# One layer of a hybrid streaming encoder: spatial products between the second gate's, attention loads for two pairs of heads, and cached rows' norms at the front

## The chip, the cores and the metric

The kernel runs on one core of one Trainium2 chip. The metric is the device time of one execution in microseconds (us). Before the change the median of three runs is 4267.01 us (4262.45 to 4268.91). TensorE does matrix products and transposes, VectorE and ScalarE work on their results, GpSimd issues the indirect gathers, and SyncE (SP) issues all other DMAs in one queue. TensorE's clock is granted at one of two levels, 1.2 and 2.4 GHz; the profile gives the granted clock as a share of the higher one.

## The reference

The layer takes 1024 new positions of a prompt stream (eight tiles of 128 rows) and 16 new positions of each of eight running streams (a ninth tile). All is float32, with a width of 1024. Cut to what matters here:

```python
h = rmsnorm(x, g_mix)
c_q, c_kv, k_r, z_u, z_v, z_ga, z_gb = split(h @ w_in)
# A: attention with 16 heads; keys of a running stream: 256 cached rows and 16 new ones
k_nope = rmsnorm((ckv_all @ w_uk).reshape(B, Sk, 16, 64), g_kn)
o_a = attend(q, k_nope, k_rope, ckv_all @ w_uv) @ w_oa
# B: spatial gating over chunks of 128 positions, 8 channel groups
u, v_g = gelu(z_u), rmsnorm(gelu(z_v), g_gm)
mixed = einsum('gts,bcsgd->bctgd', tril(w_s), v5) + b_s
o_b = (u * mixed) @ w_ob
x = x + (sigmoid(z_ga) * o_a + sigmoid(z_gb) * o_b) @ w_o
x = x + cross_attend(rmsnorm(x))          # 256 memory rows, 4 heads
x = x + peer_ffn(rmsnorm(x))              # 8 heads pick 16 of 16384 experts each
```

A prompt tile attends to its own tile and the tiles before it. In the last step each row scores two sets of 128 keys per head, takes the best 16 pairs, and sums the picked experts.

## The kernel before, in words

**Groups and stages.** The nine tiles go through the layer in four groups: (0, 8), (1, 2), (3, 4, 5) and (6, 7); tile 8 holds the running streams. `mixer` (from L1430) runs for each group: `projections`, `attend_prompt`, for group 0 `attend_sample`, `merge`, `cross`, the latents of the next group and `pre_route`. Group 0 also computes the memory's keys and values in between (`memory`). After the last group, `dense_layer` treats tiles 2 to 5 by running all 16384 experts over them as dense products; the experts of tiles 0, 8, 1, 6 and 7 are gathered row by row by GpSimd and summed on VectorE, beside everything else.

**What sets the order.** The code is traced in program order, and a scheduler then fixes the order of each engine's queue and SP's at compile time: what stands earlier goes first, unless its inputs or tiles are not there yet by the scheduler's own estimate. At run time each queue is served strictly in its order. Work from the last group's expert choice (`route`, with its `tails`), from the gathers and from the scatter of the picks is dealt out between the products of the next group by `pump` (L181), which compares counters of planned time with a clock that each product advances (`mm`, L158). `force_route` (L218) takes a step of the route without waiting for that clock; `open` counts the routes whose query products (`ppq`) are not all out.

**Tiles.** Pools have a fixed number of places: twelve general tiles of 128x1024 (`mid`, L261), four activation tiles (`act_slot`, L285), three weight tiles of 1 MB (`weight`, L273), one tile `cqT` (`spare`, L264), and in PSUM four banks `mm`, two `tr` and two `s` (L270). A load whose place is taken waits, and so does all that stands behind it in SP's queue.

**Cached rows' norms** (`past_norms`, L457). The keys of the 8 x 256 cached rows are never stored; only the inverse norm of each of their 16 heads is. For each block of 128 rows `key_squares` (L449) makes two products of 128x512 from w_uk and the cached rows (two halves each), squares them on ScalarE and sums by head on VectorE. It is a generator; `attend_prompt` takes two of its sixteen steps with every pair of heads of group 0. The result (`own`, in the place of `cqT`) is used in `attend_sample`, which also loads the new rows' own values into that tile.

**Spatial part** (`projections`, L677 to L702). For each of eight channel groups g, one product per prompt tile with the masked spatial weights (`pmix`), scaled and shifted on VectorE into `mx` (L684, L689) and multiplied into `uT` (L691). After all eight, bT takes an activation tile, and for each of eight blocks of columns come eight products of the gate (`pg`, w_gb), a Sigmoid into a small tile (L699), eight products of the result (`po`, w_ob), and the product of the two on VectorE (L701).

**Attention of the prompt** (`attend_prompt`, L747). A unit is one head of one tile; two heads are a pair. In each step of the pipeline one unit's scores are made and its softmax is started, the probabilities of the unit two back are transposed, and the values of the pair three back are summed. `load(hp)` (L755) fetches the queries (qts), the keys of both heads (kts, two loads) and the values (vts) of one pair of heads; the next pair is asked for in the middle of a pair. `fill` deals the 64 steps of the first gate (`gate`, L704, w_ga) over the units. Group 0 has one prompt tile with one tile of keys, group 1 two with up to three.

Of the kernel before, what the change touches and what calls it, by code (L numbers as in the profile page):

```python
# [16 lines left out]
ALU = mybir.AluOpType  # L17
# [119 lines left out]
class Net:  # L137
# [319 lines left out]
    def past_norms(self):  # L457

        self.own = self.spare("own")
        self.rpast = self.own[:, :16 * H].rearrange("p (c h) -> p c h", c=16)  # L460
        wk = self.weight('w_uk', 0)

        def load(b):
            ck = self.mid("ckp", 512).rearrange("p (k t) -> p k t", k=2)
            self.dma(ck, self.A['past'][b, :, :2])
            return ck

        cks = [load(0)]
        for b in range(NST):
            if b + 1 < NST:  # L470
                cks.append(load(b + 1))
            ck = cks[b]
            for i in range(2):
                self.key_squares(self.rpast[:, 2 * b + i], ck[:, :, i * P:(i + 1) * P], wk)
                yield
        r = self.rpast
        self.nc.scalar.activation(r, r, AF.Sqrt, bias=self.eps)
        self.nc.vector.reciprocal(r, r)
# [76 lines left out]
    def projections(self, tiles, hT, lat, r):  # L555
# [108 lines left out]
        if SAMPLE in tiles:  # L664
# [9 lines left out]
            for b in range(NST):  # L674
                self.dma(trs[b * STOK:(b + 1) * STOK, :, b * STOK:(b + 1) * STOK], A['wsT'][:STOK, :, :STOK])
            nc.vector.tensor_tensor(trs, trs, bc(self.tril[:, None, :], [P, 8, P]), op=ALU.mult)
        for g in range(8):  # L677
            pm = self.psum("mm", "pmix")
# [12 lines left out]
            nc.vector.tensor_tensor(uT[:, g, :], uT[:, g, :], mx[:, :T], op=ALU.mult)  # L691
        bT = self.act_slot("bT", T)
        for c in range(4):
            wg, wo = self.weight('w_gb', c), self.weight('w_ob', c)
            for b in range(2):
                pg, po = self.psum("mm", "pg"), self.psum("mm", "po")
                self.mmT(pg[:, :T], hT, wg, b)
                sg = self.small("sg", TMAX, "row", 2)[:, :T]
                nc.scalar.activation(sg, pg[:, :T], AF.Sigmoid)  # L699
                self.mmT(po[:, :T], uT, wo, b)  # L700
                nc.vector.tensor_tensor(bT[:, 2 * c + b, :], po[:, :T], sg, op=ALU.mult)  # L701
        return bT  # L702
# [43 lines left out]

    def attend_prompt(self, tiles, oT, filler, gate):  # L747
        nc = self.nc
        ts = [t for t in tiles if t != SAMPLE]
        if not ts:  # L750
            return
        n, nk = len(ts), ts[-1] + 1
        st, ld = {}, {}

        def load(hp):  # L755
            hs = slice(2 * hp, 2 * hp + 2)
            qt = self.mid("qts").rearrange("p (h t k) -> p h t k", h=2, t=4)
            self.dma(qt[:QKD, :, :n], self.qd[:, hs, ts[0]:nk])
            kt = []
            for h in range(2):  # L760
                k = self.mid("kts").rearrange("p (t k) -> p t k", t=8)
                self.dma(k[:QKD, :nk], self.kd[:, 2 * hp + h, :nk])
                kt.append(k)
            vt = self.mid("vts").rearrange("p (t v) -> p t v", t=8)
            self.dma(vt[:, :nk], self.vd[:, :nk, hp * P:(hp + 1) * P])
            ld[hp] = qt, kt, vt

        def scores(u):
            hp, i, h = u
            if hp not in ld:  # L770
                load(hp)
            if 2 * i + h == n and hp + 1 < H // 2:
                load(hp + 1)
            qt, kt, vt = ld[hp]
            t = ts[i]
            chunks = []
            for c in range(0, t + 1, 4):
                m = min(4, t + 1 - c)
                s = self.psum("mm" if (c > 0 or (t < 4 and h)) else "s", "s")
                self.mm(s[:, :m * P].rearrange("p (t k) -> p t k", t=m), qt[:QKD, h, i, :],  # L780
                        kt[h][:QKD, c:c + m, :], start=True, stop=True)
                if c + m == t + 1:
                    nc.vector.memset(s[:64, m * P - 64:m * P], NEG)
                chunks.append(s[:, :m * P])
            st[u] = self.softmax(chunks, "pr")
# [4 lines left out]
        def values(u):  # L790
            hp, i, h = u
            if not h:
                return
            vt, t = ld[hp][2], ts[i]
            po = self.psum('tr', "pov")
# [6 lines left out]
        def fill(u):  # L802
            fill.due += 64 / len(units)
            while fill.due >= 1:
                next(gate, None)
                fill.due -= 1
            if u[1:] == (0, 0):
                next(filler, None)
                next(filler, None)

# [619 lines left out]
    def mixer(self, ctx):  # L1430
# [6 lines left out]
        groups = [list(g) for g in self.groups]  # L1437
        hT = self.head(groups[0], *self.inputs(groups[0]))
        lat = self.latents(groups[0], hT)
        for gi, tiles in enumerate(groups):  # L1440
# [4 lines left out]
            gate = self.gate(tiles, hT, sa)  # L1445
            while self.open:
                self.force_route()
            if gi == 0:
                self.memory()
            oT = self.act_slot("oT", T)  # L1450
            norms = iter(self.past_norms()) if SAMPLE in tiles else iter(())
            self.attend_prompt(tiles, oT, norms, gate)
            for _ in norms:
                pass
            if SAMPLE in tiles:
# [55 lines left out]
```

## Time and profile before

| | |
|---|---|
| Runs | 4267.01 us median (4262.45 to 4268.91) |
| Profiled execution | 4245.56 us, its span 4243.8 us |
| Mean granted clock of TensorE | 0.948 |
| TensorE busy | 3855.5 us (91%) |
| VectorE busy | 3281.3 us (77%) |
| ScalarE busy | 1466.4 us (35%) |
| GpSimd busy | 1660.5 us (39%) |
| HBM | 283 GB/s over the span |

The stages follow each other along TensorE's queue: group 0 until about 610 us, group 1 until about 1100, group 2 until about 1850, group 3 until about 2660, then the dense experts, which end near 4180, and the rest of the gathers. A busy TensorE is not one at its peak: the same product takes twice as long while the lower clock is granted. Idle time of an engine counts only where the chain that ends last runs through it.

### The profile page before, as it was taken

What the parts mean: (1) busy time and instruction counts of PE and PEld (TensorE: products, weight loads), DVE (VectorE), ACT (ScalarE), POOL (GpSimd) and SP (SyncE); (2) the same over time, 40 slices, a digit from 0 to 9 for tenths busy, and PEclk for the clock granted to TensorE, in tenths of its full rate; (3) what the DMA queues carried; (4) which work ended last, traced back from release to release, by engine and by line L of the source; (5) the groups of instructions that cost most, each with busy time, mean ns of one, the idle gap of its engine ahead of it and who ended that gap; (6) DMA issues with size and microseconds to landing.
All of it is one profiled execution on the core that took longest, in us unless ns stands there. A gap on an engine that the chain in (4) does not pass through costs nothing. (4 is left out here: it accounts for less than half of the span.)

```text
span 4243.8 us, 55015 instructions
## 1 busy us (share of the span) xinstructions
PE 3855.5 (91%) x18532; PEld 2930.3 (69%) x18532; DVE 3281.3 (77%) x7539; ACT 1466.4 (35%) x2987; POOL 1660.5 (39%) x1284
## 2 busy tenths in 40 slices
PE   8999999889997899989878887889999999999994
PEld 6856767767754566656655666667888878888883
DVE  2121138756897888789898887899999989999999
ACT  4153234162241384314156441332332332332330
POOL 0000000434434456543223332246666555666555
PEclk9997999989998999999889998899999999999997
DMA  6532465878878899897778885779999999999998
GB/s 204 176 114 72 150 211 181 332 244 316 329 271 297 287 301 354 302 350 285 244 232 255 272 290 209 270 254 368 346 363 371 342 335 356 362 346 357 359 326 329
DMA packets 456027, 1205.55 MB, mean 284 GB/s; under 512 B 48896, under 2 KB 180032, under 8 KB 432320
## 3 DMA queue, kind: packets, MB, share of 16 engines
q0 software_dynamic: 184320, 671.17, 44.0%
q1 hardware_dynamic: 271424, 530.86, 36.2%
q8 instruction: 147, 2.41, 0.2%
q14 instruction: 136, 1.11, 0.1%
HBM read 1131.04 MB, written 70.82 MB: 283 GB/s over the span
## 5 line engine op out<-in xcount | busy, mean ns | idle before, releaser
L1211 POOL DMA_INDIRECT v<-peer_v,e x640 | 879.3, 1374 | 1251.4 <-DVE dots L1228 807.9
L1211 POOL DMA_INDIRECT u<-peer_u,e x640 | 780.9, 1220 | 1320.2 <-DMA e<-ed 739.5
L1250 DVE SCALAR_TENSOR_TENSOR acc<-v,wk,acc 128x1024 f32<-128x1024 f32 x635 | 814.1, 1282 | 8.5 <-DMA v<-peer_v,e 6.5
L1228 DVE CUSTOM_DVE_ANT_0 u<-u,hx 128x1024 f32<-128x1024 f32 x640 | 776.8, 1219 | 24.4 <-DMA u<-peer_u,e 24.2
L163 PE MATMUL pu<-hh,uh 128*128 128x512 f32 x1024 | 410.7, 401 | 6.6 <-ACT uh L290 4.3
L163 PE MATMUL pd<-vl,ph 128*128 128x512 f32 x1024 | 403.8, 394 | 6.0 <-DVE vl L1345 6.0
L163 PE MATMUL pu<-hl,uh 128*128 128x512 f32 x1024 | 401.7, 392 | 0.0
L163 PE MATMUL pd<-vh,pl 128*128 128x512 f32 x1024 | 401.4, 392 | 0.0
L163 PE MATMUL pd<-vh,ph 128*128 128x512 f32 x1024 | 383.2, 396 | 11.2 <-DVE dy L1420 8.4
L290 ACT ACTIVATE vh<-v 128x512 fp32r<-128x512 f32 x256 | 161.5, 632 | 604.8 <-PE pd L163 294.9
L163 PE MATMUL pg<-hT,w 128*128 128x256 f32 (+1 forms) x1024 | 296.4, 423 | 7.5 <-ACT pr L732 4.8
L163 PE MATMUL ppq<-h3T,w 128*128 128x256 f32 (+1 forms) x1024 | 262.7, 415 | 3.6 <-ACT sc L290 2.7
L163 PE MATMUL pu<-hh,ul 128*128 128x512 f32 x1024 | 261.9, 395 | 1.9 <-DVE ul L1345 1.7
L163 PEld LDWEIGHTS ppq<-h3T,w 128*128 128x128 f32 x1024 | 195.8, 194 | 62.5 <-ACT sc L290 9.8
L163 PEld LDWEIGHTS pd<-vh,ph 128*128 128x128 f32 x1024 | 193.1, 189 | 58.3 <-DVE dy L1420 9.5
L163 PEld LDWEIGHTS pg<-hT,w 128*128 128x128 f32 x1024 | 190.1, 197 | 59.2 <-issue 13.4
L163 PEld LDWEIGHTS pd<-vl,ph 128*128 128x128 f32 x1024 | 193.5, 189 | 52.2 <-DVE vl L1345 13.1
L163 PEld LDWEIGHTS pu<-hh,uh 128*128 128x128 f32 x1024 | 193.6, 189 | 48.4 <-ACT da L1396 4.8
L163 PEld LDWEIGHTS pu<-hh,ul 128*128 128x128 f32 x1024 | 194.0, 190 | 44.6 <-DVE ul L1345 4.2
L163 PEld LDWEIGHTS pd<-vh,pl 128*128 128x128 f32 x1024 | 193.6, 189 | 40.1
L163 PEld LDWEIGHTS pu<-hl,uh 128*128 128x128 f32 x1024 | 193.6, 189 | 38.2
L163 PEld LDWEIGHTS <-sa 128*128 128x128 bf16 x1536 | 114.0, 104 | 147.0 <-DVE sa L1323 71.6
(284 smaller groups left out, 6955.8 us busy)
## 6 DMA issues: line engine op xcount, KB each, us to landing
u<-uT SPq DMA_DIRECT2D x128, 512.0 KB, 7.1
v<-peer_v SPq DMA_DIRECT2D x256, 256.0 KB, 7.2
w<-w_pq SPq DMA_DIRECT2D x32, 1024.0 KB, 7.2
gd<-stage SPq DMA_DIRECT2D x256, 128.0 KB, 4.4
dg<-gd SPq DMA_DIRECT2D x128, 256.0 KB, 7.1
w<-w_zv SPq DMA_DIRECT2D x16, 1024.0 KB, 6.4
w<-w_zu SPq DMA_DIRECT2D x16, 1024.0 KB, 7.2
w<-w_gb SPq DMA_DIRECT2D x16, 1024.0 KB, 8.1
```

Source lines behind the costliest of these rows:

```text
L163: i = self.nc.tensor.matmul(out, lhsT, rhs, **k)
L290: self.nc.scalar.activation(out, in_, AF.Copy, **k)
L1211: i = self.nc.gpsimd.indirect_dma_start(out=q, out_offset=None, in_=src, in_offset=bass.IndirectOffsetOnAxis(ap=idx, axis=0))
L1228: self.after(nc.vector.tensor_tensor_reduce(u, u, hx, 1.0, 0.0, ALU.mult, ALU.add, accum_out=dots[:, k:k + 1]))
L1250: i = nc.vector.scalar_tensor_tensor(acc, v, w[:, k:k + 1], acc, op0=ALU.mult, op1=ALU.add)
```

## The change

The norms of the cached rows become a plain function that is called before the head of the first group, right after its inputs are asked for; their tile comes from the general ones. In the attention they no longer stand between the units. Where a group has at most two prompt tiles and at most four tiles of keys (groups 0 and 1), one load of queries, keys and values covers two pairs of heads (`w = 2`); each of the four loads is then twice as large, and the next is asked for in the middle of the two pairs. In the spatial part each channel group's products are followed by the eight products of one block of the gate, whose Sigmoid goes straight into bT; the products with w_ob follow when all eight are through and multiply bT in place. bT is taken ahead of that loop, and so is the loop that forces the open routes to their end.

```diff
     def past_norms(self):
-        self.own = self.spare("own")
+        self.own = self.mid("own")
...
                 self.key_squares(self.rpast[:, 2 * b + i], ck[:, :, i * P:(i + 1) * P], wk)
-                yield
...
     def projections(self, tiles, hT, lat, r):
...
+        while self.open:
+            self.force_route()
+        bT = self.act_slot("bT", T)
         for g in range(8):
             pm = self.psum("mm", "pmix")
...
             nc.vector.tensor_tensor(uT[:, g, :], uT[:, g, :], mx[:, :T], op=ALU.mult)
-        bT = self.act_slot("bT", T)
+            if g % 2 == 0:
+                wg = self.weight('w_gb', g // 2)
+            pg = self.psum("mm", "pg")
+            self.mmT(pg[:, :T], hT, wg, g % 2)
+            nc.scalar.activation(bT[:, g, :], pg[:, :T], AF.Sigmoid)
         for c in range(4):
-            wg, wo = self.weight('w_gb', c), self.weight('w_ob', c)
+            wo = self.weight('w_ob', c)
             for b in range(2):
-                pg, po = self.psum("mm", "pg"), self.psum("mm", "po")
-                self.mmT(pg[:, :T], hT, wg, b)
-                sg = self.small("sg", TMAX, "row", 2)[:, :T]
-                nc.scalar.activation(sg, pg[:, :T], AF.Sigmoid)
+                po = self.psum("mm", "po")
                 self.mmT(po[:, :T], uT, wo, b)
-                nc.vector.tensor_tensor(bT[:, 2 * c + b, :], po[:, :T], sg, op=ALU.mult)
+                nc.vector.tensor_tensor(bT[:, 2 * c + b, :], po[:, :T], bT[:, 2 * c + b, :], op=ALU.mult)
...
-    def attend_prompt(self, tiles, oT, filler, gate):
+    def attend_prompt(self, tiles, oT, gate):
...
         n, nk = len(ts), ts[-1] + 1
+        w = 2 if n <= 2 and nk <= 4 else 1
...
-        def load(hp):
-            hs = slice(2 * hp, 2 * hp + 2)
-            qt = self.mid("qts").rearrange("p (h t k) -> p h t k", h=2, t=4)
-            self.dma(qt[:QKD, :, :n], self.qd[:, hs, ts[0]:nk])
+        def load(l):
+            hs = 2 * w * l
+            qt = self.mid("qts").rearrange("p (h t k) -> p h t k", h=2 * w, k=P)
+            self.dma(qt[:QKD, :, :n], self.qd[:, hs:hs + 2 * w, ts[0]:nk])
             kt = []
             for h in range(2):
-                k = self.mid("kts").rearrange("p (t k) -> p t k", t=8)
-                self.dma(k[:QKD, :nk], self.kd[:, 2 * hp + h, :nk])
-                kt.append(k)
-            vt = self.mid("vts").rearrange("p (t v) -> p t v", t=8)
-            self.dma(vt[:, :nk], self.vd[:, :nk, hp * P:(hp + 1) * P])
-            ld[hp] = qt, kt, vt
+                k = self.mid("kts").rearrange("p (h t k) -> p h t k", h=w, k=P)
+                self.dma(k[:QKD, :, :nk], self.kd[:, hs + w * h:hs + w * (h + 1), :nk])
+                kt += [k[:, e] for e in range(w)]
+            vt = self.mid("vts").rearrange("p (t v) -> p t v", v=P * w)
+            self.dma(vt[:, :nk], self.vd[:, :nk, l * w * P:(l + 1) * w * P])
+            ld[l] = qt, kt, vt
...
-            if hp not in ld:
-                load(hp)
-            if 2 * i + h == n and hp + 1 < H // 2:
-                load(hp + 1)
-            qt, kt, vt = ld[hp]
+            l, o = hp // w, hp % w
+            if l not in ld:
+                load(l)
+            if 2 * (n * o + i) + h == n * w and l + 1 < H // 2 // w:
+                load(l + 1)
+            qt, kt, vt = ld[l]
+            h += 2 * o
...
-            if u[1:] == (0, 0):
-                next(filler, None)
-                next(filler, None)
...
-        hT = self.head(groups[0], *self.inputs(groups[0]))
+        first = self.inputs(groups[0])
+        if SAMPLE in groups[0]:
+            self.past_norms()
+        hT = self.head(groups[0], *first)
...
-            while self.open:
-                self.force_route()
             if gi == 0:
                 self.memory()
             oT = self.act_slot("oT", T)
-            norms = iter(self.past_norms()) if SAMPLE in tiles else iter(())
-            self.attend_prompt(tiles, oT, norms, gate)
-            for _ in norms:
-                pass
+            if SAMPLE in tiles and gi:
+                self.past_norms()
+            self.attend_prompt(tiles, oT, gate)
```

## Rows read from the trace of the kernel before

**Rows 1.** Busy time, granted clock and DMA of five stretches (PEclk 1.00: 2.4 GHz), by window.

```profile
core 0: us, PE busy (x) PEld busy (x) DVE busy (x) ACT busy (x) POOL busy (x), PEclk, DMA share, GB/s
...
218.00:315.00 97.00, 92.29 (x331) 55.07 (x330) 31.11 (x81) 59.79 (x130) 0.00 (x0) 0.99 0.36 106
...
835.00:940.00 105.00, 84.24 (x444) 59.90 (x443) 48.37 (x142) 71.60 (x167) 29.19 (x26) 0.85 0.77 253
...
1306.00:1345.00 39.00, 22.27 (x85) 15.42 (x84) 37.80 (x76) 4.41 (x7) 18.70 (x16) 0.69 0.72 262
...
2700.00:4180.00 1480.00, 1452.50 (x6537) 1184.62 (x6536) 1417.17 (x1997) 444.79 (x636) 857.74 (x649) 0.99 0.94 342
...
2625.00:2650.00 25.00, 20.07 (x106) 16.86 (x104) 15.05 (x99) 5.00 (x13) 0.00 (x0) 1.00 0.06 17
```

**Rows 2.** Timeline of the start, a weight's landing, and the norms' matmuls in the attention.

```profile
3.37 0.43 SPq L257 DMA_DIRECT2D w<-w_ckv  x1
...
14.42 3.93 PE L177 MATMUL pt<-const,xn 128*128 128x128 f32 x16 [14.42 <-ACT xn L290]
...
w<-w_pq SPq DMA_DIRECT2D x32, 1024.0 KB, 7.2
...
218.18 7.03 PE L163 MATMUL pk<-w,ckp 128*128 128x512 f32 x16
225.05 1.89 PE L163 MATMUL pg<-hT,w 128*128 128x256 f32 x8
```

**Rows 3.** Group 0's attention: costliest groups, TensorE's last wait, landing of its keys.

```profile
L353 ACT ACTIVATE sq<-pk 128x512 f32<-128x512 f32 x32 | 18.0, 597 | 34.8 <-PE pk L163 17.7 <-PE s L163 17.1
...
L732 ACT ACT_TABLE_LOAD x8 | 10.3, 1283 | 0.4 <-DVE s L783 0.3
...
314.72 7.16 PE L163 MATMUL pqa<-qq,wkT 64*128 64x128 f32 x32 [0.79 <-DMA qq<-qd]
...
DMA to landing us min/median/max: 1.8/1.9/6.5
```

**Rows 4.** Group 1's attention: TensorE's waits, one late load, landing of its keys.

```profile
PE s L163 <- DMA kts<-kd: 19.8, 5, 6.7
...
876.45 0.36 SPq L257 DMA_DIRECT2D w<-w_oa  x1
...
877.32 1.10 SPq L257 DMA_DIRECT2D kts<-kd  x2
...
887.62 4.60 PE L163 MATMUL s<-kts,qts 96*128 96x256 f32 x8 [4.48 <-DMA kts<-kd]
...
DMA to landing us min/median/max: 2.1/2.3/13.2
```

**Rows 5.** TensorE's waits at the spatial products (whole run, group 2, group 3); its timeline in group 2.

```profile
PE pmix L163 <- DVE mx L684: 24.1, 7, 13.2
...
PE pmix L163 <- DVE mx L684: 16.6, 3, 13.2
...
PE pgs L163 <- DVE sa L1323: 7.1, 4, 6.1
PE pmix L163 <- DVE mx L684: 5.0, 2, 2.8
...
1332.34 7.39 PE L163 MATMUL pg<-hT,w 128*128 128x384 f32 x16
...
1340.21 0.27 PE L177 MATMUL pt<-const,efij 128*128 128x128 f32 x1
```

**Rows 6.** VectorE at the spatial products of groups 2 and 3, timeline.

```profile
1321.54 0.61 DVE L684 SCALAR_TENSOR_TENSOR mx<-pmix,gcol,bs_p 128x384 f32<-128x384 f32 x1
...
1322.55 0.55 DVE L691 TENSOR_TENSOR uT<-uT,mx 128x384 f32<-128x384 f32 x1
...
2063.85 0.29 DVE L1322 TENSOR_TENSOR so<-iotas,pk 128x256 bf16<-128x256 bf16 x1 [6.83 <-DMA pk<-pb]
```

**Rows 7.** The route's query products alone, by window: group 2's spatial products.

```profile
1306.00:1345.00 39.00, 0.00 (x0) 0.69 0.72 262
```

More of the change, by code (lines that the diff above doesn't have):

```diff
@@ L778, in scores @@
                 m = min(4, t + 1 - c)
-                s = self.psum("mm" if (c > 0 or (t < 4 and h)) else "s", "s")
+                s = self.psum("mm" if (c > 0 or (t < 4 and h % 2)) else "s", "s")
                 self.mm(s[:, :m * P].rearrange("p (t k) -> p t k", t=m), qt[:QKD, h, i, :],
@@ L793, in values @@
                 return
-            vt, t = ld[hp][2], ts[i]
+            vt, t = ld[hp // w][2][:, :, hp % w * P:], ts[i]
             po = self.psum('tr', "pov")
```

## The prediction, before the change was run

> **What bounds the kernel now.** I read the stretches first, by window. In the dense stretch, 2700 to 4180 us, TensorE is busy 1452.5 of 1480 us, and nothing of it is touched; before it, at 2625 us, GpSimd has no gather left and VectorE is idle 10 of 25 us [rows 1]. So nothing is carried across that point but the place of TensorE's chain: what TensorE's chain gains or loses before it moves the end by as much. That makes the sum one of TensorE's time, stage by stage, where it is idle or slow. Then the start and the stretch in which the norms run now [rows 2, 3]: TensorE does nothing until 14.42 us, and in the attention of group 0 it is 92.29 of 97 us busy, because the norms' products pad it. Then group 1's attention, which has no such padding: 84.24 of 105 us busy, at a granted clock of 0.85, and the longest wait is for the keys [rows 1, 4]. Then the spatial products, where TensorE waits 24.1 us in all for VectorE, 16.6 in group 2 and 5.0 in group 3 [rows 5], and what VectorE did meanwhile [rows 6]. The profiled execution took 4245.6 us, 21 us under the median of the runs (4267.0). I make the sum on its span and take the difference over to the median. A measurement of this kernel can tell about 0.2% (8.5 us) from no change.
>
> **Norms at the start.** The same 64 products (128 instructions) move from group 0's attention to the front. Sixteen take 225.05 - 218.18 = 6.87 us [rows 2], so all take 8 x 6.87 = 55.0 us, at the full clock that the start has now too. Before, TensorE waited until 14.42 us for the normalised input. The norms need only w_uk and the first cached rows: asked for where w_ckv is now, at some 3.4 to 4 us, a 1 MB weight needs 7.2 us (its median), so they start near 11 us and fill 3.4 us of the wait [rows 2]. Bounds: nothing filled (the queue is crowded with inputs) and 7.2 us (the weight lands 7.2 us into the span). **Cost: +55.0 - 3.4 = +51.6 us** (48 to 55). What covered them before was the attention; that cover is gone from here. SP's queue gets w_uk and eight loads of cached rows ahead of the latents' weights, which have 55 us to land. The tile that holds the norms now keeps one of the twelve general tiles until the cached streams' attention is over; the products it would starve are loads ahead of a TensorE that has work, so I cost it at nothing, and up to 5 us if that cover fails.
>
> **Group 0's attention without them.** From the first norm product to the first product of the cached streams it takes 314.72 - 218.18 = 96.5 us [rows 2, 3]. Left are 92.29 - 55.0 = 37.3 us of TensorE and 59.79 - 18.0 = 41.8 us of ScalarE [rows 1, 3]. ScalarE is then the longer engine, and each score waits for it through the softmax, so the floor is 42 us. The ceiling is all of TensorE's work at 1.2 GHz, 75 us. The nearest row is group 1's attention: without its key waits it took (105 - 19.8) / 71.6 = 1.19 of ScalarE's busy time [rows 1, 4]. 41.8 x 1.19 = 50 us, which I take. The loads take 1.9 us here (median) [rows 3] and come half as often, so they hide. **Gain: -46.5 us** (-22 to -54). With the norms, group 0 comes to +5 us: it moves work more than it saves any. ScalarE's floor holds sixteen table loads, eight before Exp and eight before the gate's Sigmoid, at 1.283 us each [rows 3]. The Trainium skill (ScalarE: Activation LUTs, Table sets: the hidden batching unit) wants all calls of one set done before the next and gives about 2.7 us to a switch; by that figure the floor would be 64 us and the change some 20 us worse, but the rows say 1.283 and the measurement decides.
>
> **Short loads in pairs.** Only groups 0 and 1 are short enough; groups 2 and 3 keep their loads. In group 1 a pair's keys are asked for two units ahead, and queue behind a 1 MB weight: requested at 877.32, behind w_oa, used at 887.62 after a wait of 4.48 us [rows 4]. The waits sum to 19.8 us in five places. Now one request in two remains, and it comes four units ahead. A unit takes (105 - 19.8) / 32 = 2.7 us, so the lead goes from 5 to 11 us, against the 10 us that this load took (887.62 - 877.32) and 13.2 at most. Three boundaries at 1 to 2 us leave about 4: -16 us. The granted clock of 0.85 is 30% of 105 us, 31 us, at 1.2 GHz; at most 31 - 20 = 11 of these were work, and work at half speed loses half, 5.7 us. I take back 3. **Gain: -19 us**; bounds 0 (the loads are as late as now) and -25.5. SP issues fewer requests (16 fewer per group); the bytes are the same.
>
> **Spatial products with the gate's.** Nothing is added; the gate's eight products (one per channel group) stand between the spatial ones and give VectorE time. Groups 0 and 1 wait 24.1 - 16.6 - 5.0 = 2.5 us in all, and lose that: -2.5. In group 2 VectorE reaches the first result at 1321.54, some 15 us late, being behind with gathers and with the route's tail, and is busy 37.8 of 39 us [rows 1, 6]. Two spatial and two gate products can now run before TensorE needs a bank back, about 12 us of work by the gate's 7.39 us at a mixed clock [rows 5]. That would save 12. But the route's transposes come next: TensorE takes one at 1340.21, and it needs VectorE's index work, which now stands behind eight pairs of 0.61 + 0.55 us [rows 5, 6]. With six of these moved behind it, it is ready at 1340 - 7 = 1333, and TensorE will be there at about 1318 and wait. At 1333 it has then done two gate products (10 us) for the six spatial ones (4 us) that it has yet to do. **I take -4** (0 to -16.6). Group 3 is the same with another blocker: the scatter's products wait 7.1 us for tiles that VectorE can't build until a load of the picks lands at 2063.85 [rows 5, 6]. That load doesn't come sooner, and TensorE meets its products sooner. **I take -2** (0 to -12). The forced end of the route, moved ahead of the spatial products, costs nothing: none of its query products lies in that window [rows 7], so none is left to force; were some left, each would be 16 products in a row. The fourth activation slot is then free too. Gate values written straight into the result's tile save no instruction.
>
> **Sum:** 51.6 - 46.5 - 19 - 2.5 - 4 - 2 = **-22.4 us**, 4223 on the profiled execution, **4245 us** against the median.
>
> **The rivals.**
> 1. The spatial waits vanish whole (the index work and the picks are done in time after the reordering): 12.6 + 10 more, -45, 4222 us. For it: the waits are the longest single ones there. Against: VectorE is saturated in that window.
> 2. Group 1's gain is taken up elsewhere: in 85 us instead of 105, 71.6 us of ScalarE and a DMA share of 0.77 become 0.84 and 0.95 [rows 1]; gathers then land late and hold VectorE's queue ahead of the softmax. -22.4 + 19 = -3, 4264 us.
> 3. Group 0's attention, with its padding gone, runs at 1.2 GHz: 75 instead of 50 us, +25, sum +3, 4270 us. For it: in group 1 the clock is at 0.85 where TensorE waits [rows 1]. Against: there it waits for DMAs of 10 us, here for chains of one or two. The Trainium skill (TensorE: Matmul & The Clock Gate, HAM oscillation) says that idle gaps bring the half clock and that the matmuls behind them start slow; it speaks against taking filler out of a stage.
> 4. Slower: the tiles decide. A pair of pairs needs four free tiles out of twelve (eleven in group 0). If prefetched requests must wait for tiles of the set in use, all four loads leave only after its last score, and every boundary pays the whole landing: in group 1 three of 13.2 us in place of 19.8, and no gain, 19 + 19.8 = +39 against my term; in group 0 three of 6.5, +19.5. Sum -22 + 58 = +36, 4303 us; if only group 1 pays, 4284. It decides from the point where the second keys of a set are requested after the last score of the set before. Against: of twelve tiles, four are loaded and three to five hold probabilities at that time, so three or more are free.
>
> **Chances.** The forecast 0.52 (its own range 4230 to 4258), rival 1 0.16, rival 2 0.16, rival 3 0.05, rival 4 0.11. Faster by over 0.2% takes the forecast and rival 1, a little less for the forecast's upper edge: 0.67; rivals 2 and 3 are the same: 0.21; slower 0.12. The range 4214 to 4278 leaves out rival 4 and the better half of rival 1.
>
> **What would show it.** TensorE's first product near 11 us and 55 us of norms; group 0's attention of about 50 us with ScalarE over 80% busy; key waits in group 1 of about 4 us and a clock over 0.9; no wait at a spatial product in group 1, and in groups 2 and 3 waits for index or scatter tiles instead. I am wrong where group 0's attention is over 60 us or under 45, where group 1 still waits over 15 us for keys, or where groups 2 and 3 gain over 15 us.

## The result, and the profile after

The changed kernel takes 4207.65 us, median of five runs (4196.05 to 4237.43), against 4267.01 (4262.45 to 4268.91, five runs too): a ratio of 0.9872, 95% interval [0.9832, 0.9913], which is 37 to 72 us less (55 by the ratio itself). I had forecast 22 us less. The profiled execution took 4237.43 us, the longest of the five, its span 4235.7: only 8.1 us under the span of before. So the two profiles seem to say one thing and the medians another. That is resolved first, since everything else is read from profiles.

The page of the changed kernel, its head and the granted clock over 40 slices:

```profile
span 4235.7 us, 54898 instructions
...
PE 3874.7 (91%) x18532; PEld 2949.3 (70%) x18532; DVE 3282.5 (77%) x7539; ACT 1462.5 (35%) x2985; POOL 1656.1 (39%) x1284
...
PEclk9996699999999899999898998899999999999997
```

One slice is 106 us. The 6 and 6 at the fourth and fifth are the attention over the cached streams (`attend_sample`), which the change doesn't touch. The stages, by window (columns as in [rows 1]):

```profile
275.00:318.00 43.00, 37.33 (x201) 29.52 (x199) 9.19 (x49) 40.48 (x96) 0.00 (x0) 0.93 0.57 176
318.00:493.60 175.60, 162.40 (x673) 122.06 (x672) 20.12 (x65) 45.28 (x166) 0.00 (x0) 0.60 0.21 64
...
866.00:930.00 64.00, 62.70 (x379) 48.12 (x378) 45.02 (x132) 58.62 (x139) 22.40 (x23) 1.00 0.99 323
...
1305.00:1363.00 58.00, 46.35 (x162) 28.71 (x161) 53.23 (x100) 8.53 (x15) 35.24 (x29) 0.88 0.89 332
```

Group 0's attention fell to 43 us (first line; [rows 1], 97 with the norms). Group 1's attention is at the full clock with TensorE busy throughout (third line; 0.85 and 84.24 of 105 us in [rows 1]). The streams' stage has the opposite: 175.6 us at 0.60. In the profile of before it took 144.1 us, with the same 673 matmul instructions.

**The stages over all profiles.** I took the start of the first instruction of each stage on TensorE from every trace (first scores, first `pqa`, first product with w_oa, first `pmix`, last product with w_ob, last scores) and subtracted. "Streams" runs from the first `pqa` to the first product with w_oa. The columns are the profile of before and of the change, the change run again (e5), and parts of it: norms alone (e1), loads alone (e2), spatial alternation alone (e3), loads and spatial (e4), alternation in group 2 alone (e11) and in group 1 alone (e12).

| us | before | change | e5 | e1 | e2 | e3 | e4 | e11 | e12 |
|---|---|---|---|---|---|---|---|---|---|
| to group 0's first scores | 226.8 | 274.9 | 275.8 | 277.0 | 226.9 | 224.4 | 225.7 | 227.3 | 226.6 |
| group 0's attention | 87.9 | 43.1 | 43.0 | 46.1 | 88.8 | 87.7 | 87.5 | 88.0 | 88.0 |
| streams | 144.1 | 175.6 | 165.1 | 153.9 | 157.1 | 152.4 | 170.3 | 175.6 | 163.4 |
| group 1, spatial part | 67.8 | 68.1 | 68.2 | 68.0 | 67.1 | 60.1 | 68.4 | 69.7 | 60.2 |
| group 1, attention | 94.6 | 64.5 | 63.7 | 91.0 | 63.0 | 82.5 | 62.9 | 102.0 | 80.0 |
| group 2, spatial part | 141.3 | 124.6 | 123.3 | 150.1 | 151.2 | 122.9 | 123.1 | 126.8 | 147.4 |
| group 2, attention | 188.3 | 197.5 | 195.1 | 188.3 | 187.7 | 197.5 | 194.2 | 197.3 | 188.9 |
| group 3, spatial part | 99.0 | 100.8 | 100.7 | 96.0 | 98.6 | 96.6 | 97.2 | 94.7 | 92.2 |
| span | 4243.8 | 4235.7 | 4225.0 | 4259.8 | 4229.3 | 4207.8 | 4223.2 | 4262.2 | 4234.5 |
| span less streams | 4099.7 | 4060.1 | 4059.9 | 4105.9 | 4072.2 | 4055.4 | 4052.9 | 4086.6 | 4071.1 |

The streams' row moves between 144 and 176 us with no relation to what was edited: e11, which touches only group 2 a thousand microseconds later, has 175.6, as the change has. It is the same code in all nine columns. The profiled execution of before has the shortest stage of them. Without it, the change and its repetition come to 4060.1 and 4059.9, **39.7 us under before**, inside the interval of the medians. That they agree to 0.2 us is in part luck: in the rows of the table above it they differ by 3.7 us, and what the rows leave out makes up for it. That last row is what I compare below, beside the medians, and it scatters too. Group 2's spatial part, unaltered, takes 141.3 to 151.2 us, group 1's attention 91.0 to 102.0, and what the rows leave out, code that no edit changes, comes to 3181 us (e11) to 3194 (before and e4). So only 32 of the change's 39.7 us lie in the rows that the table shows (36 in e5), and a difference under some 13 us in the last row has to be looked for in the rows of the edited stages.

### The profile page after: what moved, and what is told of

It is laid out like the page before. It is cut to its first block, busy times and chain, and to the rows that moved or that the text cites. A ratio compares the mean times of both kernels' runs of the same rounds, so it can differ in the third digit from the quotient of the medians.

```text
span 4235.7 us, 54898 instructions
## 1 busy us (share of the span) xinstructions
PE 3874.7 (91%) x18532; PEld 2949.3 (70%) x18532; DVE 3282.5 (77%) x7539; ACT 1462.5 (35%) x2985; POOL 1656.1 (39%) x1284
## 5 line engine op out<-in xcount | busy, mean ns | idle before, releaser
L163 PEld LDWEIGHTS pg<-hT,w 128*128 128x128 f32 x1024 | 193.1, 201 | 67.1 <-issue 19.4
L163 PEld LDWEIGHTS pd<-vl,ph 128*128 128x128 f32 x1024 | 192.8, 188 | 52.0 <-DVE vl L1348 13.2
L163 PEld LDWEIGHTS pd<-vh,pl 128*128 128x128 f32 x1024 | 192.9, 188 | 39.7
```

The source lines that it names most:

```text
L163: i = self.nc.tensor.matmul(out, lhsT, rhs, **k)
```

## The experiments

### One part of the change at a time

The norms alone (e1), the loads alone (e2), the spatial part alone (e3), loads and spatial part without the norms (e4), and the whole change once more (e5). Each edit is the hunks of the change's diff that belong to that part, with nothing else; their marks:

```diff
# e1
+        if SAMPLE in groups[0]:
+            self.past_norms()
-            norms = iter(self.past_norms()) if SAMPLE in tiles else iter(())
# e2
+        w = 2 if n <= 2 and nk <= 4 else 1
# e3
+            pg = self.psum("mm", "pg")
+            self.mmT(pg[:, :T], hT, wg, g % 2)
+            nc.scalar.activation(bT[:, g, :], pg[:, :T], AF.Sigmoid)
# e4: e2 and e3; e5: the whole change
```

> The norms at the front alone, the rest as before. Theory A (the clock in the cached streams' stage decides group 0): the stretch up to that stage ends within 8 us of before (the change's profile shows +3.3), the stage itself takes between 125 and 180 us by its granted clock (145 at 0.78 before, 177 at 0.60 in the profile of the change), and the executions differ among themselves by more than 20 us, where those of before differ by 6; the median lies between 20 us faster and 30 us slower. Theory B (group 0 is settled, and the rest of the change makes the gain): a stage within 5 us of before, executions within 10 us of each other, and 0 to 5 us slower.

> The attention's loads for two pairs alone. Theory A: group 1's attention gains what the profile of the change shows there beside the spatial products, 25 to 30 us, and some of it is lost again before the end: 15 to 30 us faster, with executions within 10 us of each other since group 0's filler stands where it stood. Theory B (whatever group 1 gains is waited for later, as group 3 started at the same time in both profiles): under 5 us faster.

> The spatial products between the gate's alone. Theory A: 2 to 5 us gained in group 1, 15 to 18 in group 2 by the end of its spatial part, given back to under 5 by the end of that group, nothing in group 3: 0 to 10 us faster in all. Theory B (the spatial waits are the gain that the profiled execution hides): 15 to 30 us faster.

> The change without the norms' move (loads and spatial products only). Theory A: the sum of the two parts, 20 to 40 us faster, executions within 10 us of each other; the change beats it only where the cached streams' stage has the higher clock. Theory B (the norms' move is what makes the gain of the median): under 15 us faster.

> The changed kernel once more, beside the kernel before on the same chip. Theory A (the change is the sum of its parts, -31 for the loads and -23 for the spatial products, overlapping in group 1 to -38 together, and 0 to +15 for the norms): 25 to 40 us faster than before (0.6 to 0.9%). Theory B (the parts help each other, as the first measurement of 1.28% says): 50 us or more faster. In its profile group 1's attention takes 63 to 66 us at full clock, and group 0 reaches the cached streams within 8 us of before.

Measured, each against the kernel before on the same chip: e1 4268.2 us, ratio 1.0035 [1.0008, 1.0063]; e2 4224.05, 0.9926 [0.9895, 0.9957]; e3 4227.33, 0.9946 [0.9917, 0.9974]; e4 4212.77, 0.9905 [0.9872, 0.9939]; e5 4218.92, 0.9889 [0.9862, 0.9917].

- **e1:** the norms' move costs a little, 0.08 to 0.63% (3 to 27 us), and 6.2 us by the last row of the table. One half of theory A holds: the streams' stage began 8.3 us later than before (323.0 against 314.7), as the two rows above it say. The other half fell: it wanted executions of before within 6 us of each other, and on this chip before itself went from 4229.9 to 4285.05.
- **e2:** 0.43 to 1.05% (18 to 45 us), 27.5 us by the table. Group 1's attention went from 94.6 to 63.0 us. Its window in e2:

```profile
846.00:909.00 63.00, 62.95 (x378) 47.35 (x377) 43.64 (x130) 58.28 (x137) 28.02 (x24) 1.00 1.01 341
```

TensorE has no idle time left and the full clock throughout. Theory A's 15 to 30 us holds; its executions within 10 us of each other did not come (4215.11 to 4231.11).

- **e3:** 0.26 to 0.83% (11 to 35 us), and 44.3 us by the last row. The interval leaves out theory A's 0 to 10 and holds theory B's 15 to 30, the one against my forecast. The table shows 29.0 us of it in three places: 7.7 us in group 1's spatial part, 12.1 in its attention, which the edit doesn't contain, and 18.4 in group 2's spatial part, of which 9.2 are given back in the attention behind it. Most of the other 15 us lies in stages that the edit does not reach.
- **e4:** the parts do not add up. In group 1, loads and alternation together (68.4 + 62.9 = 131.3 us) are no better than the loads alone (67.1 + 63.0 = 130.1). The whole is 0.61 to 1.28% faster (26 to 54 us), so theory A's sum holds at its upper end and theory B's under 15 us is out; the executions lie 30 us apart (4201.73 to 4231.78), not within 10.
- **e5:** 0.83 to 1.38%, 35 to 59 us, between the two theories' figures.

### Where the alternation pays: group 2 alone (e11), group 1 alone (e12)

```diff
+        alt = len(tiles) == 3        # e12: alt = tiles[0] == 1
+        if alt:
+            while self.open:
+                self.force_route()
+            bT = self.act_slot("bT", T)
         for g in range(8):
...
+            if not alt:
+                continue
```

with the change's loop where `alt` holds and that of before elsewhere.

> The kernel before, with the spatial products alternated with the gate's in group 2 alone (with the forced end of the route and bT ahead of them there). Theory A (the failed step is group 2's: TensorE does gate products in the 17 us in which it waited, at a higher clock): group 2's spatial part 120 to 130 us where it was 141, 6 to 9 us given back in the attention after it, and span less the streams' stage 8 to 15 us under the before kernel's 4099.7. Theory B (as I predicted: the transposes take the place of the wait): spatial part 135 to 141 us, gain under 5 us.

> The kernel before, with the alternation in group 1 alone. Theory A (in group 1 it pays through what follows: the gate's weights are asked for earlier, the result's products run together, and the attention behind waits less for its keys): from the first spatial product to the last product with w_ob 58 to 64 us where it was 68, the attention behind it 80 to 88 us where it was 95, span less the streams' stage 15 to 25 us under 4099.7. Theory B (as I predicted: only the waits of 2.5 us at the spatial products go): spatial part 65 to 68 us, attention 92 or more, gain under 5 us.

e11: 4245.7 us, 0.9953 [0.9925, 0.9982]; e12: 4234.73, 0.9917 [0.9880, 0.9955]. In its stages theory A came out in both: e11's group 2 takes 126.8 us in the spatial part and gives back 9.0 in the attention behind it, and e12's two stages take 60.2 and 80.0. The last row says less: e11 is 13.1 us under before, but its rows add up to what they were before (905.8 and 905.7 us; group 1, which it does not touch, took 9.3 us longer, group 2 was 5.5 shorter), so the 13.1 us lie outside its rows. The runs themselves give e11 8 to 32 us. Of e12's 28.6 us, over A's 15 to 25, 22.2 lie in group 1. TensorE's waits in group 2's spatial part and the attention behind it, in e11:

```profile
PE pt L177 <- DVE efij L1188: 6.1, 1, 6.1
PE pmix L163 <- DVE mx L689: 4.7, 1, 4.7
PE pgs L163 <- DVE sa L1343: 3.6, 1, 3.6
```

The 16.6 us at `mx` [rows 5] became 4.7, and 6.1 turned up at the transposes of the route, as forecast in kind. In size it was not. Both windows of group 1 in e12, and its waits:

```profile
779.00:839.00 60.00, 58.68 (x288) 51.96 (x287) 52.25 (x115) 6.32 (x12) 29.20 (x24) 1.00 0.96 363
839.00:919.00 80.00, 69.76 (x378) 51.83 (x378) 44.29 (x129) 58.67 (x139) 24.55 (x23) 0.91 0.85 272
```

```profile
PE s L163 <- DMA kts<-kd: 9.1, 3, 4.8
PE pg L163 <- DMA w<-w_gb: 1.3, 1, 1.3
```

The alternation also changes the order of SP's queue (four w_gb together, then four w_ob), and the key waits in the attention behind fell from 19.8 to 9.1 us in three places. That the order of the queue brings this was not tried by itself, nor was the alternation without that order. That gain and the doubled loads' are of the same waits, which can be removed only once. With both edits the spatial part itself keeps 68 us; another load is late then. The changed kernel, its wait in group 1's spatial part:

```profile
PE pg L163 <- DMA w<-w_gb: 6.6, 1, 6.6
```

It is 1.3 in e12 and 6.6 in the change (7.0 in e4, 7.7 in e5), on the same weight. In e12 and in the change it is requested 13.6 us ahead of the first `pmix` (at 765.47 and 784.17), and its first product starts 15.6 and 20.8 us after the request; what precedes it on SP's queue in the change are the doubled queries, keys and values. That these are the cause was not tried by itself.

### Why the double loads remove the waits (e7, e8)

e7 keeps single pairs and asks for the next one at the first unit of a pair, as early in units as the double loads are asked for relative to their half. e8 has the double loads, but asks for them only two units ahead, as before.

```diff
# e7, on the kernel before
-            if 2 * i + h == n and hp + 1 < H // 2:
+            if 2 * i + h == (0 if n <= 2 and nk <= 4 else n) and hp + 1 < H // 2:
# e8, on e2
-            if 2 * (n * o + i) + h == n * w and l + 1 < H // 2 // w:
+            if 2 * (n * o + i) + h == (2 * n * w - 2 if w == 2 else n) and l + 1 < H // 2 // w:
```

> The kernel before with one edit: in groups 0 and 1 the next pair of heads is asked for in the first unit of a pair instead of its middle, still one pair to a load. Theory A (what the doubled load gains is lead: four units instead of two): the waits for keys in group 1 fall from 19.8 to under 8 us, that attention takes 63 to 75 us, and the kernel is 15 to 30 us faster. Theory B (places: a pair's four tiles are asked for per two heads, and requests wait for places whatever their turn): waits over 14 us, attention over 85 us, under 8 us faster.

> The doubled loads alone, but the next two pairs are asked for two units ahead of their use, the lead of before, instead of four. Theory A (lead): three boundaries of 4 to 6 us, so 10 to 18 us of waits for keys in group 1 and the attention at 75 to 88 us. Theory B (fewer tiles and requests per head, so that loads go out as soon as places are free, whatever their turn): under 4 us of waits, attention under 68 us, as with the lead of four.

e7: 4245.56 us, 0.9955 [0.9928, 0.9983]; e8: 4242.27, 0.9941 [0.9919, 0.9964]. In group 1's attention e7 still waits 17.5 us for keys and takes 87.8 us: theory B's figures there (the stage gained 6.8 us). The whole gained more than B's under 8: 7 to 31 us by the interval, 11.6 by the last row's measure (4088.1). e8 waits 14.5 us and takes 82.2: theory A's, the lead counts. Late loads of either kernel, on the timeline, first e7:

```profile
883.19 0.35 SPq L257 DMA_DIRECT2D w<-w_oa  x1
...
884.89 1.65 SPq L257 DMA_DIRECT2D kts<-kd  x2
...
895.83 3.33 PE L163 MATMUL s<-kts,qts 96*128 96x256 f32 x6 [5.08 <-DMA kts<-kd]
```

e8:

```profile
864.36 0.33 SPq L257 DMA_DIRECT2D w<-w_ga  x1
...
865.21 1.08 SPq L257 DMA_DIRECT2D kts<-kd  x2
...
879.24 3.32 PE L163 MATMUL s<-kts,qts 96*128 96x256 f32 x6 [8.30 <-DMA kts<-kd]
```

In both, as in [rows 4], the keys are requested right behind a weight of 1 MB and used 11 to 14 us later. e7's program asks early, but its keys are on the queue at 884.89, 6.4 us behind the first use of the pair before (878.47): asking earlier in program order did not bring the request forward. That the places of the tiles hold it back, as theory B has it, fits, and was not shown by itself. So neither larger loads nor an earlier request alone does it: half the requests and twice the lead do.

### The streams' stage (e6, e9, e10)

Half of group 0's 64 gate steps are moved out of the prompt's attention into the streams' stage, two per stream block, and w_uv is asked for behind them. e6 and e9 are the change with that edit, e10 the same without the norms' move (on e4).

```diff
-            fill.due += 64 / len(units)
+            fill.due += (32 if SAMPLE in tiles else 64) / len(units)
...
+            def fill(b):
+                for _ in range(2):
+                    next(gate, None)
...
-            self.pipeline(list(range(NST)), (values, flip, scores, keys), (3, 2, 1, 0))
+            self.pipeline(list(range(NST)), (fill, values, flip, scores, keys), (0, 3, 2, 1, 0))
```

> The changed kernel with half of the first gate's products of group 0 (32 calls, 13.8 us at full clock) moved out of its attention into the cached streams' stage, two with each step; w_uv is loaded behind the steps to make room. Theory A (that stage is slow because of its granted clock, which its own thin products don't hold up): a granted clock over 0.9 there, the stage 120 to 145 us long in spite of 13.8 us more work (144 to 176 in the five profiles so far), and 15 to 40 us faster than the changed kernel beside it. Theory B (the stage is bound by its chain through ScalarE, and the clock only follows): the stage 150 us or longer, and no gain.

> The changed kernel with half of group 0's gate steps moved into the cached streams' stage, run once more beside the next one. Theory A (the stage's clock follows how densely TensorE is fed): again 15 to 30 us faster than the changed kernel, so 1.2 to 2.0% faster than the kernel before; the stage, from its first product to the first product with w_oa, 135 to 155 us at a granted clock of 0.78 or more. Theory B (the one look was a lucky execution): within 0.5% of the changed kernel's ratio of 0.989, the stage over 160 us.

> As the run beside it, but with the norms left between group 0's attention units. Theory A (the norms' move costs 6 to 7 us wherever the gate's steps stand): span less the streams' stage 5 to 9 us shorter than in the run beside it, the time 0.1 to 0.3% lower. Theory B (with half of the gate's steps gone from the attention, the norms are what fills it, and both together leave it as long as before): group 0's attention no shorter than 80 us and no gain against the run beside it.

e6: 4198.91 us, 0.9834 [0.9808, 0.9859], 20 us under the change on the same chip (4218.92). e9: 4201.73, 0.9841 [0.9803, 0.9878]. e10: 4196.96, 0.9819 [0.9781, 0.9857]. All three are faster than the kernel before. Beside the change only e6 was run, and its slowest run (4201.84) is faster than the change's fastest (4206.62); e9's interval overlaps both of the change's ([0.9832, 0.9913] and [0.9862, 0.9917]), e10's the first. e9's group 0 attention and streams' stage:

```profile
276.00:307.50 31.50, 26.43 (x142) 18.84 (x140) 8.44 (x49) 28.63 (x84) 0.00 (x0) 0.90 0.59 165
307.50:456.00 148.50, 141.30 (x737) 107.98 (x736) 20.14 (x65) 57.10 (x178) 0.00 (x0) 0.82 0.30 99
```

The stage has 64 more matmul instructions (737 against 673, two to each of the 32 gate products), and it is shorter: 148.7 us at 0.82, in e6 and in e9, where the change had 175.6 and 165.1 at 0.60 and 0.66. e6's theory A is right in direction and missed its numbers (clock over 0.9, stage to 145); e9 met its theory A in all of them. Of e10, neither theory came out: its attention takes 74.0 us (B wanted 80 or more), and what it gains until the streams (300.1 against 307.5) is gone at the first product with w_oa (455.9 against 456.2), since the streams' stage took 155.8 us at 0.77 there. Span less streams is 4.5 us shorter than e9's, a little under A's 5 to 9; the median is 0.11% lower, as A has it, but the intervals overlap: which of the two is better stays open.

## Why the prediction was wrong, point by point

Direction and bound were right: TensorE's chain, stage by stage, carried to the end. The forecast was short by two steps: the loads of group 1 and the spatial part of group 2.

**Norms and group 0's attention: +5 forecast, and right by two errors that cancel.** The start, on the timeline of the changed kernel:

```profile
13.30 57.74 PE L163 MATMUL pk<-w,ckp 128*128 128x512 f32 x128 [13.30 <-DMA ckp<-past]
72.76 1.09 PE L177 MATMUL pt<-const,xn 128*128 128x128 f32 x8 [1.72 <-ACT xn L290]
```

The 128 instructions take 57.74 us where I had 55.0, and they begin at 13.30 instead of 11, waiting for the cached rows (`ckp`) and not for the weight that I had reckoned with; so 1.1 us of the old wait is filled, not 3.4. By the first scores of group 0 the later start is 48.1 to 50.2 us (the change, e5 and e1). My +51.6 counts from the first norm product, 8.6 us earlier (218.18 against 226.8); counted from the first scores it is +43.0, so the start came 5 to 7 us dearer than forecast. The attention took 43.1 us, not 50, and gave 44.8 us where the forecast, counted so, has 37.9. It is also under the 45 that I had named as a sign of being wrong. That the sum fits is luck. Together group 0 comes to +3.3 (change), +4.1 (e5) and +8.3 (e1). ScalarE sets that stage as forecast, nearly at its floor:

```profile
L735 ACT ACT_TABLE_LOAD x9 | 11.5, 1283 | 2.0 <-DVE smx L729 1.9
L718 ACT ACT_TABLE_LOAD x8 | 10.3, 1283 | 0.1
```

Seventeen table loads are 21.8 of its 40.48 busy us, and it was idle for only 43.0 - 40.5 = 2.5 us in all. The Trainium skill (ScalarE: Activation LUTs, What ACT_TABLE_LOAD costs) adds a drain of about 1.38 us to each; seventeen of these would be, as an estimate from that figure, 23 us, and the trace has no room for them as idle time. The measurement decides, as it did in the forecast.

**Loads: right in mechanism, the size off.** The failed words are "I take back 3. Gain: -19 us; bounds 0 and -25.5". Group 1's attention lost 29 to 32 us, against the 94.6 of the profile of before, in every kernel whose double loads are asked for early (unaltered it took 91.0 to 102.0). The window of 105 us that I had read for it runs 12 us past its last scores, at 928. The waits went to 1.3 us and not to 4:

```profile
PE s L163 <- DMA kts<-kd: 1.3, 1, 1.3
```

and the clock went to 1.00. My bound on the clock took the low clock to lie mostly on the waits themselves: 20 of 31 us. More of it lies behind them than that. Three stretches of group 1's attention before, each behind a wait for keys:

```profile
865.00:875.00 10.00, 10.00 (x54) 6.87 (x53) 7.48 (x22) 7.09 (x19) 3.75 (x4) 0.81 0.64 186
...
888.00:895.00 7.00, 7.00 (x28) 4.62 (x28) 3.73 (x14) 3.63 (x11) 0.94 (x1) 0.67 0.63 198
...
915.00:928.00 13.00, 13.00 (x63) 8.99 (x63) 8.01 (x24) 8.92 (x21) 3.56 (x3) 0.81 0.47 140
```

TensorE is busy through all three, and a granted clock of 0.81 means 2 x 0.19 of the stretch at 1.2 GHz: 3.8 + 4.6 + 4.9 = 13.3 us of work at half speed in these alone, more than the 11 that I allowed for all. TensorE's busy time for the stage says the same: 74.6 us before (833 to 928), 62.7 after. So the term that I had at 3 came to some 12 us, and the waits gave 18.5 where I had 16. The Trainium skill (TensorE: Matmul & The Clock Gate, HAM oscillation) says that after a wait for a DMA the next products start at the low clock; these rows agree.

**Spatial part, group 1: -2.5 forecast with group 0's, nothing gained in the change.** The waits at `mx` went, as forecast. Alone, the alternation takes 22.2 us off group 1 (e12: 7.6 in the spatial part, 14.6 in the attention), most of which I had not seen at all: a wait of 2.9 us for w_ob goes too, and half of the key waits. In the change the doubled loads have already taken the attention's part, and a wait of 6.6 us for w_gb the rest; so group 1's spatial part is where it was (67.8, 68.1).

**Spatial part, group 2: the failed step.** I wrote: "At 1333 it has then done two gate products (10 us) for the six spatial ones (4 us) that it has yet to do. I take -4." The timeline of the changed kernel, TensorE and then VectorE:

```profile
1305.83 5.33 PE L163 MATMUL pg<-hT,w 128*128 128x384 f32 x16
...
1321.62 1.02 PE L163 MATMUL pmix<-tril_p,vg 128*128 128x128 f32 x6 [4.63 <-DVE mx L686]
1322.44 6.97 PE L163 MATMUL pg<-hT,w 128*128 128x384 f32 x16
1329.24 0.83 PE L163 MATMUL pmix<-tril_p,vg 128*128 128x128 f32 x6
1329.91 4.04 PE L163 MATMUL pg<-hT,w 128*128 128x384 f32 x12
1340.96 0.47 PE L177 MATMUL pt<-const,efij 128*128 128x128 f32 x1 [7.01 <-DVE efij L1171]
...
1340.69 0.22 DVE L1171 CAST efij<-eij 128x128 f32<-128x128 int32 x1
```

VectorE was not 7 us sooner at the index work but 2.5 us later: 1340.69, where it was there at 1338.18 before:

```profile
1338.18 0.27 DVE L1168 CAST efij<-eij 128x128 f32<-128x128 int32 x1
```

What VectorE did between the first spatial result and the index work, in part, first before (1321.5 to 1338.2), then after (1320.9 to 1340.7):

```profile
L684 DVE SCALAR_TENSOR_TENSOR mx<-pmix,gcol,bs_p 128x384 f32<-128x384 f32 x7 | 4.3, 610 | 0.0
...
L1228 DVE CUSTOM_DVE_ANT_0 u<-u,hx 128x1024 f32<-128x1024 f32 x2 | 2.4, 1218 | 0.0
...
L1250 DVE SCALAR_TENSOR_TENSOR acc<-v,wk,acc 128x1024 f32<-128x1024 f32 x1 | 1.3, 1280 | 0.0
```

```profile
L1253 DVE SCALAR_TENSOR_TENSOR acc<-v,wk,acc 128x1024 f32<-128x1024 f32 x4 | 5.1, 1279 | 0.0
L1231 DVE CUSTOM_DVE_ANT_0 u<-u,hx 128x1024 f32<-128x1024 f32 x4 | 4.9, 1216 | 0.0
...
L686 DVE SCALAR_TENSOR_TENSOR mx<-pmix,gcol,bs_p 128x384 f32<-128x384 f32 x4 | 2.4, 608 | 0.0
```

Seven spatial results stood ahead of the index work and four do now, so three went behind it and not six; and the gathers' dot products (`u`) and sums (`acc`) took the time that this freed and more, 10.0 us where it was 3.7. The transposes also stand later in TensorE's queue than I put them: behind four spatial products and three and three quarters of what I called a gate product (16 instructions each), not behind two. TensorE waits 4.6 and 7.0 us there, and does gate products where it stood for 13.2 us at one stretch. At the first transpose it has 60 of the gate's instructions behind it, where it had 16 before, and 24 of the 48 spatial ones still to do, where it had none. By the rows' 5.33 us for 16 and 0.83 us for 6 that is, as an estimate, 14.7 - 3.3 = 11 us, of which 1.8 go because the transpose comes that much later in the stage (35.8 us after the first `pmix`, 34.0 before). The clock is 0.88 from 1305 to 1363, against 0.79 over the same stretch before:

```profile
1305.00:1363.00 58.00, 40.26 (x140) 25.71 (x138) 50.37 (x97) 5.67 (x10) 29.01 (x26) 0.79 0.77 277
```

The mean of the spatial part over the six profiles without the alternation in group 2 (before, e1, e2, e7, e8, e12) is 147.6 us; over the eight with it (the change, e3 to e6, e9 to e11) it is 124.1. So it gains 23.5 us.

What is given back behind it is in part the scatter's work. The scatter's products `pgs`, TensorE's busy time and count first, before and then after, in the spatial part and in the first 120 and 126 us of the attention, which hold the last of them:

```profile
1306.00:1447.00 141.00, 22.48 (x258) 16.43 (x43) 0.90 0.86 292
1447.00:1567.00 120.00, 14.11 (x126) 7.94 (x21) 0.90 0.86 281
```

```profile
1305.00:1430.00 125.00, 17.44 (x198) 12.11 (x32) 0.92 0.91 325
1430.00:1556.00 126.00, 21.79 (x186) 12.26 (x32) 0.88 0.84 273
```

Of the 384 instructions 60 moved from the spatial part into the attention, and 7.7 us of TensorE's time with them (21.79 - 14.11). The attention's means are 187.9 us without and 197.3 with the alternation, 9.4 more. The net is 14 us where I had 4, near the end of my bounds (16.6); both parts together take 317 to 325 us with the alternation and 330 to 339 without. The profile of before, on which I had made the sum, is the shortest of the six without it, so against that one alone the net is 7.5 us (the change) and 11.2 (e5).

**Group 3: -2 forecast,** nothing gained (99.0, 100.8 and 100.7): the scatter's tiles are what is waited for, as forecast.

**The sum,** with these sizes: norms +5, loads -31, group 2 -14, the rest 0, is -40, against -39.7 by the table and, by the ratio of the medians, -55 [-72, -37] in the first measurement and -47 [-59, -35] in its repetition (e5). The close fit to the table is in part luck, since of its 39.7 us only 7.5 are group 2's and 7.5 lie outside its rows. Against the median of before, -40 is 4227 us, still inside my range of 4214 to 4278; the 15 us between 40 and 55 lie within the intervals, and no profile shows where they are. Of the rivals, the first (the spatial waits vanish) came true in part: they did not vanish; in group 2 the 16.6 us became 4.6 there and 7.0 at the transposes, with work between, and a wait of the scatter's products behind them stayed (3.5 us, 5.0 before). Rival 2 fell: the DMA share is 0.99 in group 1's attention, above my 0.95, and the stages behind don't pay for it: group 2's of e2, 151.2 and 187.7 us, lie within 0.7 us of the span of the others that lack the alternation. Rival 3 fell in its place (0.93 in group 0's attention). Rival 4 fell (waits of 1.3 us). I also leaned on a profile of before with a short streams' stage; the 21 us between it and the median, which I took over, are of the size of that; which stage was longer in the runs without a profile is not known.

## What to carry to other kernels

A wait costs more than its own length: count the work behind it that runs at the low clock, by windows that contain no wait, before the removal is priced. Two edits that remove the same wait are worth it once, and each must be timed alone to see that. Time that an edit frees on a busy engine goes to what stands next in its queue: look for that before you count on something being ready sooner. Before two profiles are compared, look for a stage that differs between executions of the same code; take it out, or the difference of the spans tells of it and not of the change, and look in the rows of the edited stages for what is left.

## What was not expected of the hardware

The streams' stage ran the same 673 instructions in 144 to 176 us, and its granted clock went with the time (0.78 and 0.60). TensorE's idle time in it is 12.9 to 14.5 us in all eleven profiles that have these instructions. The waits in it are the same, first before, then after:

```profile
PE pol L163 <- ACT ol L290: 5.1, 14, 0.4
PE pt L177 <- ACT unit L290: 4.7, 4, 1.9
```

```profile
PE pol L163 <- ACT ol L290: 5.1, 14, 0.4
PE pt L177 <- ACT unit L290: 5.3, 4, 1.9
```

Two stretches of 15 us, the first from before and the second from after:

```profile
345.00:360.00 15.00, 13.33 (x83) 9.85 (x82) 2.87 (x9) 5.32 (x19) 0.00 (x0) 1.00 0.40 126
```

```profile
390.00:405.00 15.00, 14.22 (x71) 12.37 (x72) 0.00 (x0) 3.98 (x18) 0.00 (x0) 0.50 0.08 32
```

TensorE is busy in 14.22 of 15 us at 1.2 GHz in the one, and in 13.33 at 2.4 GHz in the other: in this stage of thin products (most of 128 columns) the busy share does not tell the clock. With 64 instructions of 256 columns spread through it the granted clock was 0.82 in two profiles (0.77 in the one without the norms' move), and the stage was among the shortest, though these take 21.8 us of TensorE's time themselves (e9). Why one execution falls to 0.60 and another doesn't, no run here shows.

Loads of keys, which land in 2.3 us (median, [rows 4]), were used, after a wait, only 10 to 14 us behind their request when this stood right behind that of a weight of 1 MB while gathers ran; e2's doubled loads land in 11.5 us (median), and no wait shows, because they are asked for that much earlier.
